# First attention layer: the small term of k's normalization is added to k's squares by GpSimd and VectorE instead of by a second TensorE product

## The chip, the cores and the metric

The kernel runs on one core of a Trainium2 chip. A core has five engines with queues of their own, which wait for each other through semaphores: TensorE (PE in the profile, its weight loads PEld), VectorE (DVE), ScalarE (ACT), GpSimd (POOL) and SyncE (SP), which here issues the DMAs. The metric is the device time of one execution in microseconds; a kernel's time is the median of its runs.

## The reference: what is computed

Four layers over 1040 tokens (16 learned ones and 1024 given) of width 1024: attention over a sliding window, mLSTM, HGRN2, and attention again. Each layer normalizes its input, projects it, mixes it along the sequence, gates the result and projects it back. What matters here is the beginning of an attention layer:

```python
def rmsnorm(x, g):
    xf = x.astype(jnp.float32)
    y = xf * lax.rsqrt(jnp.mean(xf * xf, axis=-1, keepdims=True) + EPS)
    return (y * g.astype(jnp.float32)).astype(x.dtype)
...
    q, k, v, z = _split(u @ w_in, (A_W, A_KVW, A_KVW, A_W))
    q = rope(rmsnorm(q.reshape(bsz, lp, A_HEADS, A_HD), q_gain), pos)
    k = rope(rmsnorm(k.reshape(bsz, lp, A_KV, A_HD), k_gain), pos)
    v = v.reshape(bsz, lp, A_KV, A_HD)
    o = sliding_window_attention(q, k, v, sinks, valid)
```

`u` is the normalized input, so each token's row of it has a factor 1/sqrt(m + EPS), m the mean of the squares of the token's 1024 values. There are 16 heads of q and 4 of k and v, 64 wide. q and k are normalized once more for each head, which takes the token's factor out again except in the small term: with k computed from the input without the token's factor, the mean of k's squares over a head has EPS (m + EPS) added instead of EPS.

## The kernel before

The values lie transposed, 128 channels on the partitions and tokens along the row; `x` has eight such tiles. Tokens are worked in three chunks of 400, 384 and 256. A product of two float32 matrices is made as three products of split values (`uh`, `ul` of the input, `wh`, `wl` of the weights), so one projection of 128 outputs and one chunk is 24 products (L233) that accumulate in one bank `pj`. Weights come by DMA into `wr` (L209), are split by ACT (`wh`, L197) and DVE (`wl`, L198).

The first layer doesn't wait for its own normalization. `Scale.unit` multiplies the input by the gain alone, and the projections start. `Scale.squares` adds up the squares of `x` over the eight tiles in `acc`, one row `r` of the whole length, and `Scale.sums` makes from it, with a product by ones (`pr`), the token's factor, which goes to DRAM (`dram[0]`) for the gates, and EPS m, the small term of the title, which is kept in `acc` and goes to DRAM too (`dram[1]`, tile name `scaled`, L443).

The two tiles of k (two heads each) are made by `qk_proj` with t None. The first tile stands at the layer's head, after the first two tiles of q; the second one (called with fetched=True) stands among the attention units, at some 225 us. For each chunk: `evac` reads the projection out of `pj` with ACT, once with the gain (dst, L577) and once squared (sq, L578); `turned` issues four DMAs that copy quarters of dst, turned by 32 partitions, into a third tile `rot` (L571); `stat` multiplies sq by a mask of ones for each head (L617), which gives every partition the sum of its head's 64 squares, and in this layer adds the small term with a second product (L620), a row of ones with one partition times the row e; `rstd_from` makes 1/sqrt of it on ACT with a logarithm and an exponential (L344, L345); `rope` turns dst with the factors `cs` on DVE (L627 to L631), and `k_split` splits the result (L510 to L513).

For the first tile e is row 0 of `acc`. For the second tile, `acc` being gone, `early` has row 0 of `rot` filled with e from DRAM (L565) while the projection runs, and `turned` comes in `stat`, behind the second product, since it overwrites that row.

The attention then runs in units of one block of 128 queries, two heads: `S_step` (products `pm`, L729 and L730, then a masked maximum on DVE, L737, an exponential on ACT, L740, a reciprocal on DVE, L742, and a multiplication on GpSimd, L743), `T_step` two units later on PE (transposition `pt`, L758) and `V_step` (products `po`, L776). Projections of the next tiles are woven between these steps.

The order on PE is that of a list of steps which the program writes: each step has a cost, and the delays in tables such as `D_K0` and `D_K1` say how long after the end of its projection a step is put in (ns of the list's costs). The order on the other engines is made by a scheduler from the program's order and its own estimates; `hi` gives a step a higher priority there. SP issues its DMAs strictly in its queue's order.

## Time and profile before

| | |
|---|---|
| runs, median (lowest to highest) | 2572.62 us (2570.91 to 2580.6), 3 runs |
| the profiled execution | 2572.24 us, of it the span 2570.4 us |
| PE busy | 2525.0 us, 98% of the span |
| DVE, ACT, POOL busy | 2029.8, 1747.3, 247.6 us |
| granted TensorE clock, mean | 0.999 |
| first layer | from 0 to about 479 us, when the second layer's first products start |
| first k tile, mask products (L617) | at 30.4, 47.1 and 59.4 us |
| first attention unit (L729) and first transposition (L758) | at 63.6 and 67.3 us |
| second k tile, mask products | at 230.7, 236.8 and 243.4 us |

A row of the timeline gives the start in us from the span's start, the duration, engine, line, operation, the names and the shapes; in brackets behind it stands how long the engine was idle before it and what it waited for. Groups of rows give a count, the busy time, the mean duration in ns and the idle time in front. The small product of float32 values appears as two instructions (x2), since it is run in parts. A matmul's end is modelled, and products overlap, so starts are compared and not durations.

### The profile page before, as it was taken

What the parts mean: (1) busy time and instruction counts of PE and PEld (TensorE: products, weight loads), DVE (VectorE), ACT (ScalarE), POOL (GpSimd) and SP (SyncE); (2) the same over time, 40 slices, a digit from 0 to 9 for tenths busy, and PEclk for the clock granted to TensorE, in tenths of its full rate; (3) what the DMA queues carried; (4) which work ended last, traced back from release to release, by engine and by line L of the source; (5) the groups of instructions that cost most, each with busy time, mean ns of one, the idle gap of its engine ahead of it and who ended that gap; (6) DMA issues with size and microseconds to landing.
All of it is one profiled execution on the core that took longest, in us unless ns stands there. A gap on an engine that the chain in (4) does not pass through costs nothing. (4 is left out here: it accounts for less than half of the span.)

```text
span 2570.4 us, 55467 instructions
## 1 busy us (share of the span) xinstructions
PE 2525.0 (98%) x20614; PEld 2476.9 (96%) x20614; DVE 2029.8 (79%) x5602; ACT 1747.3 (68%) x4699; POOL 247.6 (10%) x572
## 2 busy tenths in 40 slices
PE   9999999999999999999999999999999999999999
PEld 8899989999999999999999999999999998999999
DVE  7897898786767676767677788988878888887896
ACT  8766766676565656565675758877676857767772
POOL 0321231000000000000000000110010000321320
PEclk9999999999999999999999999999999999999999
DMA  5223212022222212121221111111111013212112
GB/s 158 63 66 89 60 50 70 30 54 54 48 53 47 50 50 46 53 47 46 50 50 53 56 42 35 35 35 35 43 35 42 27 52 97 61 49 78 55 43 77
DMA packets 103344, 140.27 MB, mean 55 GB/s; under 512 B 15369, under 2 KB 58514, under 8 KB 103074
## 3 DMA queue, kind: packets, MB, share of 16 engines
q1 hardware_dynamic: 103074, 136.73, 19.6%
q8 instruction: 162, 2.65, 0.5%
q14 instruction: 108, 0.88, 0.1%
HBM read 121.83 MB, written 4.27 MB: 49 GB/s over the span
## 5 line engine op out<-in xcount | busy, mean ns | idle before, releaser
L233 PE MATMUL pj<-uh,wh 128*128 128x384 f32 (+2 forms) x2688 | 901.2, 335 | 6.8 <-ACT uh L403 6.3
L233 PE MATMUL pj<-ul,wh 128*128 128x384 f32 (+2 forms) x2688 | 863.5, 321 | 0.3
L233 PE MATMUL pj<-uh,wl 128*128 128x384 f32 (+2 forms) x2688 | 863.0, 321 | 0.0
L233 PEld LDWEIGHTS pj<-uh,wh 128*128 128x128 f32 x2688 | 507.0, 189 | 14.4 <-ACT uh L403 6.3
L233 PEld LDWEIGHTS pj<-ul,wh 128*128 128x128 f32 x2688 | 507.5, 189 | 4.3 <-DVE ul L198 0.9
L233 PEld LDWEIGHTS pj<-uh,wl 128*128 128x128 f32 x2688 | 506.5, 188 | 0.0
L198 DVE TENSOR_TENSOR wl<-wr,wh 128x512 fp32r<-128x512 f32 (+1 forms) x338 | 234.2, 704 | 71.0 <-ACT wh L197 68.5
L197 ACT CAST wh<-wr 128x512 fp32r<-128x512 f32 (+1 forms) x338 | 203.4, 613 | 92.3 <-PE pj L328 34.6
L328 PE MATMUL pj<-yh,wh 128*128 128x384 f32 (+2 forms) x768 | 252.9, 329 | 10.2 <-DVE x L331 8.3
L331 DVE TENSOR_TENSOR x<-x,pj 128x384 f32<-128x384 f32 (+2 forms) x480 | 234.6, 510 | 34.4 <-PE pj L328 33.1
L328 PE MATMUL pj<-yl,wh 128*128 128x384 f32 (+2 forms) x768 | 245.9, 320 | 0.0
L328 PE MATMUL pj<-yh,wl 128*128 128x384 f32 (+2 forms) x768 | 245.8, 320 | 0.0
L283 PE MATMUL pj<-wh,uh 128*128 128x256 f32 (+1 forms) x768 | 222.0, 289 | 0.6 <-DVE kwl L1051 0.6
L283 PE MATMUL pj<-wl,uh 128*128 128x256 f32 (+1 forms) x768 | 216.2, 282 | 0.0
L283 PE MATMUL pj<-wh,ul 128*128 128x256 f32 (+1 forms) x768 | 215.7, 281 | 0.0
L740 ACT ACTIVATE Sm<-Sm,s 128x257 f32<-128x257 f32 (+2 forms) x272 | 131.1, 483 | 88.5 <-DVE s L737 85.8
L743 POOL TENSOR_TENSOR Sm<-Sm,s 128x512 f32<-128x512 f32 (+2 forms) x136 | 139.3, 1025 | 402.9 <-DVE s L742 381.0
L460 ACT ACTIVATE t<-t 128x384 f32<-128x384 f32 (+2 forms) x240 | 118.2, 493 | 66.9 <-DVE t L459 65.5
L197 ACT CAST yh<-r 128x384 fp32r<-128x384 f32 (+2 forms) x120 | 56.9, 479 | 152.3 <-PE pj L328 136.4
L328 PEld LDWEIGHTS pj<-yh,wh 128*128 128x128 f32 x768 | 144.5, 188 | 14.3 <-DVE x L331 10.5
L283 PEld LDWEIGHTS pj<-wh,uh 128*128 128x128 f32 x768 | 144.6, 188 | 1.5 <-DVE kwl L1051 0.9
L328 PEld LDWEIGHTS pj<-yl,wh 128*128 128x128 f32 x768 | 144.6, 188 | 0.6 <-DVE yl L198 0.2
(332 smaller groups left out, 5688.0 us busy)
## 6 DMA issues: line engine op xcount, KB each, us to landing
wr<-in_b_win SPq DMA_DIRECT2D x124, 256.0 KB, 2.9
wr<-in_a_win SPq DMA_DIRECT2D x80, 256.0 KB, 2.8
wr<-in_c_win SPq DMA_DIRECT2D x64, 256.0 KB, 2.8
wr<-in_a_wout SPq DMA_DIRECT2D x32, 256.0 KB, 2.9
rw<-rowsd SPq DMA_DIRECT2D x64, 128.0 KB, 4.7
wr<-in_b_wout SPq DMA_DIRECT2D x32, 256.0 KB, 2.8
t<-t SPq DMA_DIRECT2D x100, 48.0 KB, 1.9
cs<-in_rope SPq DMA_DIRECT2D x11, 400.0 KB, 3.5
```

The lines of the kernel that those rows point to most:

```text
L197: s.copy(h, src)
L198: v.tensor_tensor(l, src, h.bitcast(F32), op=ALU.subtract)
L233: pe.matmul(acc[:, :cn], a[:, k, :], b[:, k, c0 : c0 + cn], start=(k == 0 and i == 0), stop=(k == KT - 1 and i == 2))
L283: pe.matmul(acc[:cn, :nc], a[:, k, c0 : c0 + cn], m[:, kk, :], start=(k == 0 and j == 0), stop=(k == KT - 1 and j == 2))
L328: pe.matmul(acc[:, :cn], a[:, k, mc], b, start=(k == 0 and i == 0), stop=(k == 1 and i == 2))
L331: v.tensor_tensor(x[:, m, c0 : c0 + cn], x[:, m, c0 : c0 + cn], acc[:, :cn], op=ALU.add)
L460: s.activation(a[:, :cn], a[:, :cn], AF.Exp)
L740: s.activation(Sm[:nq, u, : nk + 1], Sm[:nq, u, : nk + 1], AF.Exp, scale=-1.0, bias=st[:nq, u : u + 1], accum_out=den[:nq, u : u + 1])
L743: g.tensor_tensor(Sm[:nq, :, :nk], Sm[:nq, :, :nk], den[:nq].rearrange("p (u c) -> p u c", c=1).to_broadcast([nq, 2, nk]), op=ALU.mult)
```

## The change

The second product goes. `sums` now writes EPS m, without the factor 64, into all 128 rows of `acc` instead of one, and the term is added to the squares before the mask product, which sums 64 of them. A new step `bounded` does that: for the first tile GpSimd adds `acc` to sq; for the second tile the row is read from DRAM into all 128 partitions of `rot`, DVE adds it to sq, and `turned` follows the add, no longer the products. `D_EPS` puts this step 2600 ns and 300 ns behind the projection, ahead of `stat`; for the second tile it has the higher priority. The cost of `stat` in the list is halved, which shifts what is woven around it.

```diff
+D_EPS = 2600.0, 300.0
...
                 pe.matmul(pr[:, :cn], ones, acc, start=True, stop=True)
-                s.activation(acc[0:1], pr[0:1, :cn], AF.Identity, scale=64 * EPS / D)
+                s.activation(acc, pr[:, :cn], AF.Identity, scale=EPS / D)
...
             def early(n, c0, cn):
                 late[n] = work(n, c0, cn)
-                sp.dma_start(late[n][2][0:1], scale.dram[1, c0 : c0 + cn])
+                sp.dma_start(late[n][2], scale.dram[1, c0 : c0 + cn].partition_broadcast(P))
...
                     st = psa()
-                    pe.matmul(st[:, :cn], R["masks"][:, 0:P], sq, start=True, stop=not scaled)
-                    if scaled:
-                        e = late[n][2] if fetched else scale.row[:, c0 : c0 + cn]
-                        pe.matmul(st[:, :cn], ones[0:1], e[0:1], start=False, stop=True)
+                    pe.matmul(st[:, :cn], R["masks"][:, 0:P], sq, start=True, stop=True)
+                    rstd_from(st, sq, cn, 64, scale.eps2 if scaled else eps)
+
+                def bounded():
+
+                    sq = late[n][1]
                     if fetched:
+                        v.tensor_tensor(sq, sq, late[n][2], op=ALU.add)
                         turned(n)
-                    rstd_from(st, sq, cn, 64, scale.eps2 if scaled else eps)
+                    else:
+                        g.tensor_tensor(sq, sq, scale.row[:, c0 : c0 + cn], op=ALU.add)
...
-                return [(d[0], [(8 if scaled else 4) * cn * MM, stat, None]), (d[1], [0.0, rope, None]), (d[2], turn)]
+                res = [(d[0], [4 * cn * MM, stat, None]), (d[1], [0.0, rope, None]), (d[2], turn)]
+                return [(D_EPS[fetched], [0.0, hi(bounded) if fetched else bounded, None])] + res if scaled else res
```

On DVE, at the first attention unit (`pm_848` and `Sm_849` are its products and its probabilities, ISA its maximum, `qs` q's split parts, `v` parts of v, `wl` weights), there stood before:

```order
L530 TENSOR_TENSOR qs_786<-Ph_669,qs_786 64x256
L737 ISA Sm_849,s_851<-pm_848,masks_186,cons_188,rq_404 16x16
L737 ISA s_851 16x1
L690 SCALAR_TENSOR_TENSOR v_833<-pt_824,scale,v_833 128x128
L737 ISA Sm_865,s_867<-pm_864,masks_186,cons_188,rq_404 16x16
L737 ISA s_867 16x1
L737 ISA Sm_849,s_851<-pm_848,masks_186,cons_188,rq_415 16x16
L737 ISA s_851 16x1
L690 SCALAR_TENSOR_TENSOR v_836<-pt_824,scale,v_836 128x128
L737 ISA Sm_865,s_867<-pm_864,masks_186,cons_188,rq_415 16x16
L737 ISA s_867 16x1
L742 RECIPROCAL s_852<-s_852 16x2
```

And in the changed kernel, from the same place on:

```order
L743 ISA Sm_849,s_851<-pm_848,masks_186,cons_188,rq_405 16x16
L743 ISA s_851 16x1
L743 ISA Sm_849,s_851<-pm_848,masks_186,cons_188,rq_416 16x16
L743 ISA s_851 16x1
L531 TENSOR_TENSOR qs_794<-Ph_669,qs_794 64x256
L696 SCALAR_TENSOR_TENSOR v_833<-pt_824,scale,v_833 128x128
L199 TENSOR_TENSOR wl_785<-wr_790,wh_784 128x512
L696 SCALAR_TENSOR_TENSOR v_836<-pt_824,scale,v_836 128x128
L748 RECIPROCAL s_852<-s_852 16x2
L531 TENSOR_TENSOR qs_797<-Ph_669,qs_797 64x256
```

The first unit's maxima moved ahead of the q splits, the second unit's (`Sm_865` before) went behind the first one's reciprocal, and a weight split stands ahead of that reciprocal, where it was the row after it.

On SP, in the second k tile (`scaled` is the row of the small term, t with 32 rows the turned quarters, `wr` weights, `cs` the rope factors), the queue was before:

```order
L587 DMA cs_3196<-in_rope 128x2x400
L565 DMA t_3161<-scaled 1x384
L571 DMA t_3111<-t_3109 32x400 x2
L571 DMA t_3161<-t_3159 32x384 x3
L571 DMA t_3111<-t_3109 32x400
L209 DMA wr_3422<-in_a_win 128x512
L209 DMA wr_3426<-in_a_win 128x512
L587 DMA cs_3258<-in_rope 128x2x384
L565 DMA t_3209<-scaled 1x256
```

And now:

```order
L588 DMA cs_3206<-in_rope 128x2x400
L572 DMA t_3111<-t_3109 32x400 x4
L566 DMA t_3166<-scaled 128x384
L210 DMA wr_3417<-in_a_win 128x512
L210 DMA wr_3421<-in_a_win 128x512
L588 DMA cs_3268<-in_rope 128x2x384
L572 DMA t_3166<-t_3164 32x384 x4
L566 DMA t_3214<-scaled 128x256
```

The row for a chunk now stands behind all four turned quarters of the chunk before, and the read of the rope factors stands ahead of the third row as it did.

## The prediction

> **What bounds the kernel now.** I read the page first, then the waits of TensorE (PE) in the stretch where both k tiles are made, then the stretches around them, then the rows of the removed product.

> ```profile
> span 2570.4 us, 55467 instructions
> PE 2525.0 (98%) x20614; PEld 2476.9 (96%) x20614; DVE 2029.8 (79%) x5602; ACT 1747.3 (68%) x4699; POOL 247.6 (10%) x572
> ```

> PE is busy for 98% of the span, so 45.4 us are all that could be won by removing waits; work taken from PE itself counts where PE does not stand still right after it. Between 20 and 480 us PE waits mostly for transpositions, and once in the second k tile:

> ```profile
> PE pt L758 <- POOL Sm L743: 7.7, 8, 2.2
> ...
> PE pa L617 <- ACT t L578: 1.5, 1, 1.5
> ```

> By stretches (columns: us, busy us of PE, PEld, DVE, ACT, POOL, then the granted clock):

> ```profile
> 20.00:62.00 42.00, 41.91 (x263) 38.23 (x262) 33.45 (x76) 37.74 (x103) 1.17 (x7) 1.00 0.38 106
> ...
> 68.70:72.10 3.40, 3.07 (x16) 2.78 (x15) 2.10 (x6) 2.32 (x6) 1.08 (x3) 0.50 0.81 239
> ```

> While the first k tile is made (20 to 62 us), PE is the bound: 41.91 of 42.00 us. ACT with 37.74 and DVE with 33.45 are close behind, and will not follow all of what PE gains. The granted clock is 0.50 from 68.7 to 72.1 us, after the first long wait of PE, which costs some 1.7 us of the 3.4.

> **The six products removed.** The first chunk of the first k tile, and the same step in the last attention layer, which has no second product and is followed by the same 384 columns:

> ```profile
> 30.36 0.83 PE L617 MATMUL pa<-r,masks 128*128 128x400 f32 x2
> 31.12 0.93 PE L620 MATMUL pa<-r,ones 1*128 1x400 f32 x2
> 31.98 0.44 PE L233 MATMUL pj<-uh,wh 128*128 128x384 f32 x1
> 32.26 0.34 PE L233 MATMUL pj<-ul,wh 128*128 128x384 f32 x1
> ...
> 2135.12 0.83 PE L617 MATMUL pa<-r,masks 128*128 128x400 f32 x2
> ...
> 2135.97 0.34 PE L233 MATMUL pj<-ul,wh 128*128 128x384 f32 x1
> ```

> From the start of the mask product to the second projection product it takes 32.26 - 30.36 = 1.90 us with the second product and 2135.97 - 2135.12 = 0.85 without: 1.05 us. The same for 256 columns, the third chunk of the second k tile against the last layer:

> ```profile
> 243.39 0.70 PE L617 MATMUL pa<-t,masks 128*128 128x256 f32 x2 [1.53 <-ACT t L578]
> 244.02 0.69 PE L620 MATMUL pa<-t,ones 1*128 1x256 f32 x2
> ...
> 244.92 0.34 PE L233 MATMUL pj<-ul,wh 128*128 128x384 f32 x1
> ...
> 2155.55 0.59 PE L617 MATMUL pa<-r,masks 128*128 128x256 f32 x2
> ...
> 2156.15 0.33 PE L233 MATMUL pj<-ul,wh 128*128 128x384 f32 x1
> ```

> 1.53 - 0.60 = 0.93 us. With 1.0 between them for 384 columns, a tile gives 1.05 + 1.0 + 0.93 = 3.0 us, both 6.0. The lower bound takes only the distance from one product's start to the next, 31.12 - 30.36 = 0.76 and 244.02 - 243.39 = 0.63, with 0.7 between: 2.1 a tile, 4.2 in all. I take 3.0, as those rows have the same neighbours. Writing all 128 rows at L442 instead of one keeps the number of columns; I cost it at nothing.

> **The add on GpSimd (first tile).** GpSimd's adds in the trace, and one beside DVE work:

> ```profile
> L743 POOL TENSOR_TENSOR Sm<-Sm,s 128x512 f32<-128x512 f32 x112 | 124.2, 1109 | 259.3 <-DVE s L742 239.5 <-PE pt L758 5.9 <-DVE rq L605 5.1
> ...
> L743 POOL TENSOR_TENSOR Sm<-Sm,s 128x288 f32<-128x288 f32 x16 | 11.1, 694 | 131.9 <-DVE s L742 129.8 <-PE pt L758 2.0
> ...
> 223.28 1.40 POOL L743 TENSOR_TENSOR Sm<-Sm,s 128x512 f32<-128x512 f32 x1 [5.01 <-DVE s L742]
> ...
> 223.89 1.77 DVE L530 TENSOR_TENSOR qs<-t,qs 64x384 fp32r<-64x384 f32 x2
> ...
> L530 DVE TENSOR_TENSOR qs<-t,qs x90: 418/553/1297, 35.5 to 2441.2; 64x384 fp32r<-64x384 f32 x46, 64x256 fp32r<-64x256 f32 x30, 64x400 fp32r<-64x400 f32 x14
> ```

> Between 694 ns (288 columns) and 1109 ns (512), 400 columns take about 0.90 us, 384 about 0.87, 256 about 0.63. Side by side the two engines hold each other up: 1.40 us instead of 1.11 for GpSimd, 0.89 each instead of 0.55 for DVE, so one such add can cost DVE 2 x 0.34 = 0.7 us. [...] Does PE wait for the add? The tightest chunk is the third:

> ```profile
> 55.63 0.36 ACT L578 ACTIVATE r<-pj 128x256 f32<-128x256 f32 x1
> ...
> 59.38 0.59 PE L617 MATMUL pa<-r,masks 128*128 128x256 f32 x2
> ```

> The square ends at 55.99, the add 0.63 later at 56.6, and PE, some 2.05 us earlier after two removed products, comes at 57.3. 0.7 us are left, or 0.4 with the 0.3 us of contention. Cost 0, as long as that cover holds.

> **What the first tile's 3.0 us are worth.** The next thing PE waits for is the first transposition of probabilities, and its chain runs over DVE, ACT and GpSimd:

> ```profile
> 67.32 0.39 PE L758 MATMUL pt<-ident,Sm 128*16 128x128 f32 x2 [2.17 <-POOL Sm L743]
> ...
> 75.48 0.66 PE L758 MATMUL pt<-ident,Sm 128*128 128x128 f32 x4 [0.94 <-POOL Sm L743]
> ...
> 46.45 0.17 DVE L605 SCALAR_TENSOR_TENSOR rq<-pa,scale 128x6 f32<-128x6 f32 x1 [2.39 <-PE pa L600]
> ...
> 63.59 0.87 DVE L530 TENSOR_TENSOR qs<-Ph,qs 64x256 fp32r<-64x256 f32 x2
> ...
> 66.51 0.66 DVE L198 TENSOR_TENSOR wl<-wr,wh 128x512 fp32r<-128x512 f32 x1
> ```

> DVE last waited long for PE at 46.45 us, and there PE is one product (1.05 us) earlier; from then on DVE is nearly full, so it comes forward by 1.05 us, not by 3.0. In the new order the two maxima of the first unit stand ahead of the q splits (0.87 us), but a weight split (0.66 us) now stands ahead of the reciprocal: 1.05 + 0.87 - 0.66 = 1.26 us earlier, so the transposition runs at about 66.1. PE would be there at 67.32 - 2.17 - 3.0 = 62.2 and waits 3.9 us instead of 2.17. Behind it up to the third transposition (75.48) PE has as many rows as before, and the third unit's maxima now go ahead of the splitting of k's last chunk, so of its wait of 0.94 us all may go: 1.26 + 0.94 = 2.2 us. Bounds: 0 (GpSimd's add beside DVE eats the 1.26) and the whole 3.0. I take 2.2. That the wait leaves the clock low is nothing new: it was at 0.50 for 3.4 us already.

> **What the second tile is worth.** SP's queue and the chunks' squares:

> ```profile
> 225.12 0.38 SPq L565 DMA_DIRECT2D t<-scaled  x1
> ...
> 236.99 0.25 SPq L565 DMA_DIRECT2D t<-scaled  x1
> ...
> 238.84 2.43 SPq L571 DMA_DIRECT2D t<-t  x4
> ...
> 243.96 0.38 SPq L587 DMA_DIRECT2D cs<-in_rope  x1
> ...
> 235.29 0.57 DVE L627 TENSOR_TENSOR t<-t,cs 128x400 f32<-128x400 f32 x1 [3.63 <-DMA t<-t]
> ...
> 227.20 0.50 ACT L578 ACTIVATE t<-pj 128x400 f32<-128x400 f32 x1
> ...
> 242.95 0.38 ACT L578 ACTIVATE t<-pj 128x256 f32<-128x256 f32 x1
> ...
> t<-scaled SPq DMA_DIRECT2D x8, 200.0 KB, 3.3
> t<-scaled SPq DMA_DIRECT2D x8, 192.0 KB, 3.1
> t<-scaled SPq DMA_DIRECT2D x8, 128.0 KB, 3.0
> ```

> The row is now spread over 128 partitions, 200 KB for the first chunk; such transfers exist in the gate projections and land after 3.0 to 3.3 us. On the old clock: issued at 225.12, landed 228.4, later than the square (227.7); the add takes a DVE operation of this size (0.57), 229.0. Only then do the four turning transfers go (2.43 us of SP), and behind them in the queue the next chunk's row: 231.4, landed 234.5, added 235.1, turned 237.5; the third row goes at 237.5, lands 240.5, is added at about 241.0. PE, two products earlier, is at the third mask product at 243.39 - 1.53 - 2.05 = 239.8 and waits 1.3 us to 241.1. Before it went at 243.39 because the square (242.95) needed a buffer that the first chunk's k held; that chunk is done sooner, since all its turning transfers no longer wait for PE to read the row out of the same tile. So 243.39 - 241.1 = 2.3 us, and 0.93 for the third product: 3.2. Bounds: 3.0 + 1.5 = 4.5 if no wait is left, 0.9 if the third chunk is not released sooner than now. The three adds on DVE (1.5 us) are covered by its wait of 3.63 us in this stretch; with that cover gone they would sit ahead of the rope work of k, which nobody needs for several us.

> **Sum.** 2.2 + 3.2 = 5.4 us off the profiled execution, whose own time is 2572.24 us (span 2570.4 and 1.8 around it), 0.4 under the median of the runs, 2572.62. That gives 2566.8 on its clock and 2567.2 as a median; I say 2567.

> **Rivals.** 1. All of it counts: 6.0 us of products, 1.5 of the wait at 243.39, and the first transposition follows PE because DVE's chain was itself paced by PE. 2572.6 - 7.5 = 2565, and 2564 with the 0.94 of the third transposition. For it speaks PE's 41.91 of 42.00 us; against it ACT's 37.74 in that stretch. 2. The gain turns into waits: the first transposition stays at 67.3 because GpSimd's adds hold DVE up (0.7 us each), and the third chunk's row lands no earlier than its square came; what is left is about 1 us, 2571.5. [...] 3. Slower: the spread row is held in SP's queue. Ahead of the third row stands the read of the rope factors for the chunk before, and such a read was held until 243.96 us here. If it were so held now, the four turning transfers (2.4) and the row (3.0) would put the add at about 249.8 and the mask product at 249.9: 6.5 us later than now, less 0.93 and the first tile's 2.2, 3.4 us slower, 2576. It decides from an issue of the third row after about 243.1 us; now it is 236.99. 4. That the change doesn't do what it says can be left out: the order has no second product, three adds on GpSimd and three on DVE.

> **How the numbers follow.** A measurement of this kernel tells some 0.5% (13 us) from no change; every case lies inside. Forecast 0.55 (its own range 2564 to 2570), all of it 0.13, turned into waits 0.18, slower 0.14. The range 2562.5 to 2574 leaves out the slower case and the far end of the first rival, under 0.2. Beyond 0.5% on either side I see only what I have not thought of, 0.03 and 0.03.

> **What would show it.** Mask product to second projection product in 0.85 us for 400 columns; the first transposition near 66 us with a wait near 3.9; the third mask product of the second tile near 243.4 - 2.2 - 2.3 = 238.9 us, waiting for a DVE add; from 480 us on no difference in length. Wrong would make it: a mask product of the first tile waiting for GpSimd, SP's third spread row issued after the 243 us mark, or new waits of PE among the units of the first pair.

## The result, and the profile after

The changed kernel takes 2581.77 us (median of 14 runs) where the kernel before takes 2575.40 (14 runs of the same measurement): a ratio of 1.0023, 95% interval 1.0016 to 1.0030. It is slower by some 6 us, where 2567 was forecast. Of all runs on record two were far slower than the others, one of the kernel before (2933.55 us) and one of the second experiment's (7708.59 us); no ratio and no mean below holds them.

The page of the changed kernel, first its span and busy times, then TensorE's waits from 20 to 480 us (us in all, times, longest):

```profile
span 2578.6 us, 55434 instructions
PE 2525.7 (98%) x20602; PEld 2481.9 (96%) x20602; DVE 2035.2 (79%) x5605; ACT 1747.0 (68%) x4699; POOL 250.5 (10%) x575
```

```profile
PE pt L764 <- POOL Sm L749: 6.8, 7, 2.2
PE pa L618 <- DVE t L625: 4.0, 2, 2.7
PE pm L735 <- DVE Pl L767: 4.0, 2, 2.5
...
PE pa L436 <- ACT r L345: 1.1, 1, 1.1
```

Six products are gone, and yet PE is busy for 0.7 us longer than before (2525.7 against 2525.0) and idle for more besides. Where that comes from is seen in the granted clock, the column behind POOL's. These are stretches of 3.41 us of the changed kernel, in pairs: one in which PE waited long, and the one right behind it (columns as in the prediction: us, busy us of PE, PEld, DVE, ACT, POOL, the granted clock, then the DMA's share and GB/s).

```profile
63.40:66.81 3.41, 1.18 (x13) 0.98 (x12) 3.08 (x14) 3.41 (x15) 0.46 (x2) 1.00 0.25 76
66.81:70.22 3.41, 3.41 (x19) 3.27 (x18) 2.40 (x12) 2.32 (x11) 0.42 (x2) 0.50 0.56 158
240.89:244.31 3.42, 1.21 (x7) 1.19 (x8) 1.81 (x4) 2.15 (x6) 0.00 (x0) 1.00 0.83 246
244.31:247.72 3.41, 3.41 (x14) 3.22 (x14) 1.15 (x3) 3.05 (x8) 0.00 (x0) 0.50 0.14 38
329.64:333.06 3.42, 0.89 (x5) 0.57 (x5) 3.30 (x8) 1.52 (x5) 1.46 (x2) 1.00 0.41 138
333.06:336.47 3.41, 3.41 (x15) 3.39 (x14) 2.76 (x10) 1.10 (x4) 0.42 (x1) 0.50 0.03 7
401.32:404.74 3.42, 1.34 (x12) 1.13 (x11) 3.36 (x10) 3.37 (x11) 1.14 (x1) 1.00 0.03 8
404.74:408.15 3.41, 3.41 (x17) 3.41 (x18) 2.44 (x9) 2.33 (x8) 0.36 (x2) 0.50 0.02 5
2445.91:2449.32 3.41, 1.25 (x9) 0.98 (x8) 3.32 (x8) 1.01 (x4) 1.09 (x2) 1.00 0.01 2
2449.32:2452.73 3.41, 3.41 (x15) 3.41 (x14) 2.53 (x8) 0.00 (x0) 0.00 (x0) 0.50 0.00 0
```

Five times PE works at half clock (0.50) for 3.41 us and loses some 1.7 us each time, an estimate that takes half of the 3.41 us; the profile of before shows this once. The starts of the five, 66.81, 244.31, 333.06, 404.74 and 2449.32 us, lie 52, 26, 21 and 599 times 3.413 us apart: a grid that holds over these 2382.51 us, 698 times 3.413. One 3.413 us stretch of it is called a field here. The wait of about 2.1 us near 400 us stands in both kernels. In the changed one it falls into one field of the grid (2.08 us of idle time) and the next field is at half clock; in the kernel before a border of the grid cuts it into 1.11 and 0.98 us, and the clock stays at 1.00:

```profile
396.40:399.81 3.41, 2.30 (x20) 2.10 (x18) 3.28 (x12) 3.35 (x10) 0.21 (x1) 1.00 0.21 37
399.81:403.23 3.42, 2.44 (x20) 2.44 (x21) 3.25 (x11) 3.02 (x9) 1.11 (x2) 1.00 0.02 5
```

In the five fields ahead of the half-clock stretches PE was idle for 2.08 to 2.53 us.

The grid doesn't stand at the same place in every execution: counted from the span's start, a border lies at 68.72 us in the profile of before and at 66.81 in that of the changed kernel, 1.91 us apart, which is less than a field. And the executions of one kernel don't lose the same: the mean granted clock of the 14 runs of the changed kernel lies between 0.993 and 0.998. What all runs have is the mean granted clock c of the span. The time lost to the half clock is put at (1 - c) times the span, and the rest at what the kernel would take at full clock. Means over the runs of each kernel (over all kernels of this document the standard error is 0.4 to 1.1 us for the lost time and 0.3 to 0.6 for the last column; c is known to three digits in each run):

| kernel | mean us | lost to half clock | at full clock |
|---|---|---|---|
| before (33 runs, first experiments) | 2576.5 | 5.3 | 2571.2 |
| changed (14 runs) | 2582.0 | 10.9 | 2571.1 |

By this reckoning the change is worth nothing at full clock, and it doubles what the half clock takes, by 5.6 us. That is the result in two numbers; the experiments have to say why.

The reckoning is good to 1 or 2 us. The kernel before has no c on record for its 14 runs beside the changed kernel; their mean is 2575.7, 0.8 under that of the 33. And within one kernel, over the 221 runs of this document with a c, a run that lost 1 us more by c was only 0.74 us longer (standard error 0.04; the rounding of c explains a part of what is missing to 1). At that price 4.1 of the 5.5 us between the two rows are the half clock's, and the change costs 1.4 us at full clock.

### The profile page after: what moved, and what is told of

The parts are those of the page before. It is cut to its first block, busy times and chain, and to the rows that moved or that the text cites. A ratio compares the mean times of both kernels' runs of the same rounds, so it can differ in the third digit from the quotient of the medians.

```text
span 2578.6 us, 55434 instructions
## 1 busy us (share of the span) xinstructions
PE 2525.7 (98%) x20602; PEld 2481.9 (96%) x20602; DVE 2035.2 (79%) x5605; ACT 1747.0 (68%) x4699; POOL 250.5 (10%) x575
## 4 chain that ended last, share of the span: by engine, by line
PE 76%; DVE 10%; ACT 8%; DMA 3%; issue 2%; POOL 0%; SPq 0%; DVEq 0%; ACTq 0%; POOLq 0%
PE pj L234 37%; PE pj L329 16%; PE pj L284 9%; PE po L1015 2%; PE po L782 2%; PE pt L764 1%; DVE wl L199 1%; ACT Sm L746 1%; DVE Sm L743 1%; PE pm L1358 1%; ACT wh L198 1%; PE pm L735 1%; PE pm L736 1%; DMA rw<-rowsd 1%; PE pj L280 1%
## 5 line engine op out<-in xcount | busy, mean ns | idle before, releaser
L234 PEld LDWEIGHTS pj<-uh,wh 128*128 128x128 f32 x2688 | 508.0, 189 | 12.8 <-ACT uh L404 6.6
L198 ACT CAST wh<-wr 128x512 fp32r<-128x512 f32 (+1 forms) x338 | 203.1, 613 | 91.1 <-PE pj L329 33.8
L198 ACT CAST yh<-r 128x384 fp32r<-128x384 f32 (+2 forms) x120 | 56.9, 479 | 153.3 <-PE pj L329 139.1
L329 PEld LDWEIGHTS pj<-yh,wh 128*128 128x128 f32 x768 | 145.1, 189 | 12.8 <-DVE x L332 7.7
## 6 DMA issues: line engine op xcount, KB each, us to landing
rw<-rowsd SPq DMA_DIRECT2D x64, 128.0 KB, 4.5
```

Source lines behind the costliest of these rows:

```text
L198: s.copy(h, src)
L234: pe.matmul(acc[:, :cn], a[:, k, :], b[:, k, c0 : c0 + cn], start=(k == 0 and i == 0), stop=(k == KT - 1 and i == 2))
L329: pe.matmul(acc[:, :cn], a[:, k, mc], b, start=(k == 0 and i == 0), stop=(k == 1 and i == 2))
```

## The experiments

Three theories were in question. A: the new order costs the time. The mask product's step is entered in the list at cost 4 instead of 8, so the interleaving of the projections with the attention steps shifts in many places. B: the second tile's spread rows and adds cost it. C: a long wait costs a half-clock stretch beside itself, and whether it does depends on the grid. The tables give means as above; ratios are those of the measurement, each against the kernel before.

**1. The adds in the old order.**

```
-  res = [(d[0], [4 * cn * MM, stat, None]), ...
+  res = [(d[0], [(8 if scaled else 4) * cn * MM, stat, None]), ...
```

> The changed kernel with one number put back: the step of the mask product is again entered in the list with the cost of two products (8 instead of 4 per column), so TensorE's instructions stand in the order of the kernel before, but without the second products and with the three GpSimd and three VectorE adds. Theory A (the new order costs the time): waits at 330 us and 620 us go, TensorE's idle time from 260 to 700 us falls from 15.9 us back to about 12, and the time is 1 to 4 us below the kernel before. Theory B (the second tile's rows and adds cost the time, the order is harmless): the two waits for VectorE's adds near 235 and 240 us stay at 1.3 and 2.7 us, and the time stays 4 to 7 us above the kernel before. Theory C (clock gate): whatever the time, every stretch at half clock is 3.41 us long, all of them lie on one grid of 3.413 us, and each follows a grid window in which TensorE stood idle for 2.0 us or more.

Measured: 2576.96 us, ratio 1.0005 (0.9996 to 1.0013). TensorE's waits from 20 to 480 us:

```profile
PE pa L618 <- DVE t L625: 3.1, 2, 2.0
PE pm L735 <- DVE x L332: 1.7, 1, 1.7
```

With the old order no loss clear of the noise is left, so A holds as to sign; but the gain of 1 to 4 us that A expected isn't there in the time. The wait near 330 us is back at 1.66 us, that for VectorE's adds stays (3.1 us), and the idle time from 260 to 700 us is 12.8 us, close to the 12 of before. Its profile has five half-clock stretches on one grid, each behind a field with 1.92 to 2.21 us of idle time, so the 2.0 of C was set too high. At full clock the kernel is at 2569.2, 2.0 under before; the half clock takes 7.7 instead of 5.3.

**2. The new order alone.**

```
-  (d[0], [(8 if scaled else 4) * cn * MM, stat, None])
+  (d[0], [4 * cn * MM, stat, None])          # in the kernel before
```

> The kernel before with that one number changed (cost 4 instead of 8): six second products as before, no adds, one-row reads, but TensorE's order of the changed kernel. Theory A: 4 to 8 us slower than the kernel before, with a wait above 2.2 us near 330 us and one near 620 us. Theory B: within 2 us of the kernel before, third mask product of the second tile waiting some 1.5 us or less. Theory C as above: half-clock stretches only after grid windows with at least 2.0 us of idle time.

Measured: 2582.11 us, ratio 1.0023 (1.0013 to 1.0033), the same as for the whole change and inside A's 4 to 8 us. One number of the list, with no instruction added or removed on TensorE, costs what the change costs. The row near 330 us in the kernel before, and here:

```profile
330.28 0.39 PE L729 MATMUL pm<-r,qs 128*128 128x256 f32 x1 [1.68 <-DVE x L331]
```

```profile
335.37 0.58 PE L729 MATMUL pm<-r,qs 128*128 128x256 f32 x1 [2.52 <-DVE Pl L761]
```

In the new order the step of the scores (S) stands one projection step earlier there. It waits for VectorE, which comes no sooner, so 0.85 us of covered waiting turn into an open wait; and 2.52 us are enough for a half-clock stretch where 1.68 were not: in the profiles of the five kernels with the second tile's new cost (the changed one, experiments 2, 4, 5 and 9) the wait is 2.5 us, and a half-clock stretch begins each time within 1 us of the wait's end; in the other eight it is 1.6 to 1.7 us and none begins there.

A second place lies near 160 us. The changed kernel's VectorE has a row of a gate (L479) between the two maxima (L743) for which a transposition waits, 1.22 us; in the kernel before the two maxima (L737) stand together, and the wait is 0.17 us:

```profile
159.09 0.54 DVE L743 CUSTOM_DVE_ANT_0 Sm<-pm,masks,cons 128x256 f32<-128x256 f32 x1
...
159.55 0.56 DVE L479 TENSOR_TENSOR r<-r,t 128x384 f32<-128x384 f32 x1
160.02 0.54 DVE L743 CUSTOM_DVE_ANT_0 Sm<-pm,masks,cons 128x256 f32<-128x256 f32 x1
```

```profile
160.75 0.54 DVE L737 CUSTOM_DVE_ANT_0 Sm<-pm,masks,cons 128x256 f32<-128x256 f32 x1
...
161.21 0.54 DVE L737 CUSTOM_DVE_ANT_0 Sm<-pm,masks,cons 128x256 f32<-128x256 f32 x1
```

It is so in all kernels in which the first tile has cost 4, and also in the tenth experiment, where TensorE's order is the old one: this place hangs on VectorE's order, which a scheduler makes, and so only in part on the cost. At full clock the order costs 1.3 us (2572.5), by the half clock 4.5 more (9.8 lost).

The wait near 620 us that A named isn't there: its 2.25 us stood in the profile of the changed kernel alone, and no other kernel's profile has more than 1.21 us at that place.

**3. The change on the first tile alone.**

```
-  sp.dma_start(late[n][2], scale.dram[1, c0 : c0 + cn].partition_broadcast(P))
+  sp.dma_start(late[n][2][0:1], scale.dram[1, c0 : c0 + cn])   # row 64 times as large
 ...
+  if scaled and fetched:
+      pe.matmul(st[:, :cn], ones[0:1], late[n][2][0:1], start=False, stop=True)
+      turned(n)
```

> The change on the first k tile alone: GpSimd adds there, the second tile has its one-row read and its second product as before (the row in DRAM is written 64 times as large by one small ACT operation per chunk). Theory A: still slower or even, since half of the order's change is in it, -1 to +3 us. Theory B: the first tile gains what three products are worth, 2 to 3 us faster than the kernel before, no wait for a VectorE add at 235 and 240 us.

The step has cost 4 for the first tile and 8 for the second here. Measured: 2576.83 us, ratio 1.0007 (0.9997 to 1.0017). As far as the time goes, A's range holds it and B's does not. At full clock it is level with the first experiment (2568.8 against 2569.2; 2.4 under before), but it loses 9.2 us to the half clock. One of its waits is for GpSimd's add itself:

```profile
47.98 1.21 POOL L633 TENSOR_TENSOR r<-r,r 128x384 f32<-128x384 f32 x1 [17.89 <-ACT r L581]
```

```profile
49.24 1.65 PE L620 MATMUL pa<-r,masks 128*128 128x384 f32 x2 [2.38 <-POOL r L633]
```

ACT makes the second chunk's square some 6 us later here than in the changed kernel, the add comes after it, and PE stands in front of the mask product; a half-clock stretch starts at 49.13 us.

**4. The change on the second tile alone.**

```
-  pe.matmul(st[:, :cn], R["masks"][:, 0:P], sq, start=True, stop=True)
+  pe.matmul(st[:, :cn], R["masks"][:, 0:P], sq, start=True, stop=not scaled or fetched)
+  if scaled and not fetched:
+      pe.matmul(st[:, :cn], ones[0:1], scale.row[0:1, c0 : c0 + cn], start=False, stop=True)
```

> The change on the second k tile alone: spread rows and VectorE adds there, the first tile has its second product (the row in DRAM is written 1/64 as large by one small ACT operation per chunk). Theory A: 0 to +4 us. Theory B: 6 to 9 us slower than the kernel before, with waits for VectorE's add near 1.3 us at the second and 2.7 us at the third chunk, the third spread row landing 3.9 us after its issue as in the changed kernel.

The step has cost 8 for the first tile and 4 for the second here. Measured: 2579.51 us, ratio 1.0012 (1.0004 to 1.0021). The waits for VectorE's add are 1.68 and 2.71 us (B: 1.3 and 2.7), but the loss is 3 us and not 6 to 9; A's 0 to 4 holds it. At full clock 2573.5, 2.3 over before: what the first tile gains (2.4) the second loses, each with its part of the new order in it.

**5. The new order without the adds.**

```
-  v.tensor_tensor(sq, sq, late[n][2], op=ALU.add)
   turned(n)
-  else: g.tensor_tensor(sq, sq, scale.row[:, c0 : c0 + cn], op=ALU.add)
-  sp.dma_start(late[n][2], scale.dram[1, c0 : c0 + cn].partition_broadcast(P))
```

> The changed kernel, in its own order, with the small term left out of k's squares altogether: no adds on GpSimd or VectorE and no spread rows for the second tile (so k's factor lacks the entry's small term; the rest is computed as before). Theory A (the order costs 5 to 6 us, the six products are worth about what the second tile's waits take back): the two waits at 235 and 240 us (4.0 us together) go, the wait of 2.5 us near 330 us stays; 2 to 5 us under the changed kernel, so between the kernel before and 4 us above it. Rival (the adds cost nothing on the path): within 1 us of the changed kernel, some 6 us above the kernel before.

Measured: 2581.85 us, ratio 1.0016 (1.0008 to 1.0025). In microseconds the median is that of the changed kernel, but the kernel before was slower in this measurement: against it the loss is 4.7 us, over A's 0 to 4 and under the rival's 6. So the time decides neither; the parts say more. At full clock it is 2.3 under before, where the changed kernel is 0.1 under, so the adds and rows do cost some 2 us on the path; but it loses 11.7 us to the half clock. Its profile has the wait near 330 us (2.51), the third transposition's (2.15, as in the second experiment), and, since PE no longer waits in the second tile, 1.80 us at v's transposition behind it, at 247.7 us; the changed kernel has less than 0.8 at the last two. Work taken away ahead of a wait came out as a longer wait.

**6. Idle products in the kernel before.**

```
+  for _ in range(FILL[first].get((w["pair"], b, w["hh"]), 0)):
+      pe.matmul(pt[:, 0, 0, :], ident, ident, start=True, stop=True)
   for ki, (kb, ko, _) in enumerate(kbs):      # the transpositions
```

> The kernel before with 12 idle products of TensorE (identity by identity, 128 columns, into the tile that the transpositions then overwrite), placed ahead of three transpositions for which TensorE waits about 2 us each: 5 at 65 us, 4 at 399 us, 3 at 2181 us. Theory C (a grid window of 3.41 us with about 1.9 us or more of idle time is followed by one at half clock): no half-clock stretch at 68, 400 or 2184 us in any execution; the waits become 0.6 to 0.9 us shorter each with the transposition at the same time; median 1.5 to 4 us under the kernel before. Rival (the half clock costs nothing, or does not follow from the idle time): no change, or up to 1 us slower by the added products.

Measured: 2575.91 us against 2577.16, ratio 0.9993 (0.9984 to 1.0001). Smaller than expected, and the interval just reaches no change. The profile has no half-clock stretch at the three filled places; it has others (75.0, 245.7, 2153.7, 2447.3 us). The transposition runs at 67.34 us, where it ran at 67.32 without the products, with half the wait:

```profile
65.00 1.27 PE L754 MATMUL pt<-ident 128*128 128x128 f32 x10
67.34 0.39 PE L762 MATMUL pt<-ident,Sm 128*16 128x128 f32 x2 [1.06 <-POOL Sm L744]
```

The lost time falls from 5.5 us to 3.7, and at full clock nothing changes (2571.5 both).

**7. The same, with the adds in the old order.** As the sixth, on the first experiment's kernel, and ahead of the second tile's mask products:

```
   st = psa()
+  for _ in range((0, 4, 3)[n] if fetched else 0):
+      pe.matmul(st[:, :P], ident, ident, start=True, stop=True)
   pe.matmul(st[:, :cn], R["masks"][:, 0:P], sq, start=True, stop=True)
```

> The adds in the order of the kernel before (the first experiment's kernel), with idle products ahead of the first transposition (6), the second and third mask product of the second k tile (4 and 3), and the transpositions at 397 us (4) and in the last attention layer (3). Theory C: the half-clock stretches at 65, 236, 400 and 2185 us go and only one near 2444 us can remain; 3 to 6 us under the kernel of the first experiment, so 2571 to 2574 where the kernel before has 2576.7. Rival: no change against the first experiment.

Measured: 2572.11 us against 2577.16, ratio 0.9985 (0.9976 to 0.9994): 4.9 us under the kernel of the first experiment. The lost time falls from 7.7 to 3.3 us. The profile has one half-clock stretch that C didn't want, right behind a wait of 2.43 us at the third mask product that three products didn't fill.

**8. The second tile's rows read by GpSimd's queue.**

```
-  sp.dma_start(late[n][2], scale.dram[1, c0 : c0 + cn].partition_broadcast(P))
+  g.dma_start(late[n][2], scale.dram[1, c0 : c0 + cn].partition_broadcast(P))
```

> The first experiment's kernel with the second tile's three spread rows read by GpSimd's queue instead of SP's, where they stand behind the four turning transfers of the chunk before and ahead of weights and rope factors. Theory (SP's queue sets the chain): the rows land before the squares, the waits of 1.96 and 1.18 us at the second and third mask product fall to under 0.5 us each, and the time is 1 to 4 us less than in the first experiment. Rival (the spread transfer itself, or the release of its buffer, sets the chain): waits as before, no change in time.

Measured: 2580.00 us, ratio 1.0014 (1.0005 to 1.0023), and not the gain of the theory. The rival had the cause, the release of a buffer, though not the waits, which move into one:

```profile
PE pa L618 <- DVE t L625: 6.1, 1, 6.1
```

```profile
233.84 0.54 POOL L566 DMA_DIRECT2D t<-scaled  x1 [5.42 <-DVE t L634]
```

```profile
241.11 0.39 ACT L579 ACTIVATE t<-pj 128x256 f32<-128x256 f32 x1 [1.80 <-DVE t L634]
242.18 0.42 DVE L625 TENSOR_TENSOR t<-t,t 128x256 f32<-128x256 f32 x1
```

The wait at the second mask product is gone, and the third has all of it and more. The third row goes only when VectorE's rope work (L634) frees its buffer, and the third chunk's square waits for the next such release, in turn for the rope factors of the chunk before. So SP's queue set the second chunk's time, and in this kernel the six temporary buffers set the third's.

**9. Idle products in the changed kernel.** As the seventh, in the new order, with 5, 2, 6, 4 and 3 products.

> The changed kernel, in its own order, with idle products ahead of the first transposition (5), the second and third mask product of the second k tile (2 and 6), the transposition at 403 us (4) and the first one of the last attention layer (3). The wait of 2.5 us at 330 us, which comes from the order, can't be filled in this way and stays. If half-clock stretches after long waits are a part of the changed kernel's loss: 3 to 5 us under the changed kernel, so 0 to 3 us above the kernel before, with half-clock stretches left at 333 us (in most executions) and near 2449 us. Rival (the order's loss is all plain waiting): within 1 us of the changed kernel, 5 to 6 us above the kernel before.

Measured: 2577.83 us against 2578.88, ratio 0.9992 (0.9983 to 1.0001), where the changed kernel had 1.0023. By the ratios twenty idle products take back 0.3% or 8 us, more than the 3 to 5 expected (by the means, each against its own kernel before, 7.1). They bring the changed kernel level, within the noise, with the filled kernel before of the sixth experiment (0.9992 and 0.9993; 20 and 12 idle products): with most of the long waits filled, no loss by the change is left. The lost time falls from 10.9 to 6.1 us, below that of the kernel before in this measurement (6.8). The wait that the order made stays, and so does the half-clock stretch behind it, at 333.19 us:

```profile
332.29 0.39 PE L738 MATMUL pm<-r,qs 128*128 128x256 f32 x1 [2.52 <-DVE Pl L773]
```

**10. The first tile alone, in the old order, filled.** The third experiment's kernel with cost 8 for both tiles and 6, 3, 4 and 3 idle products.

> GpSimd's adds on the first k tile alone, in the order of the kernel before (cost 8 kept for both tiles), the second tile with its one-row read and second product, and idle products ahead of the first transposition (6), the third mask product of the second tile (3), the transposition near 399 us (4) and the first one of the last attention layer (3). If the first tile's three products are worth 2.6 us, as the first experiment's trace has it, and the second tile's 1.2: 2570 to 2573 where the kernel before has 2577, within 1.5 us of the seventh experiment. Rival (the gain of the seventh experiment came from the second tile): 2574 or more.

Measured: 2574.74 us against 2578.88, ratio 0.9986 (0.9977 to 0.9995). As a ratio it equals the seventh. In microseconds it falls in the rival's range (2574 or more); but the kernel before was at 2578.9 and not at 2577 in this measurement, and 4.1 us under it is the near edge of the 4 to 7 expected. So the time alone doesn't settle it. At full clock it is 2.0 under before.

**11. More idle products in the seventh.**

```
-  for _ in range((0, 4, 3)[n] if fetched else 0):
+  for _ in range((0, 5, 7)[n] if fetched else 0):
```

> The seventh experiment's kernel with 5 and 7 instead of 4 and 3 idle products at the second and third mask product of the second k tile, where its trace still had a wait of 2.43 us and a half-clock stretch right behind it. Theory C: that stretch goes in all executions, which is worth 0.57 x 1.7 = 1 us over the seventh experiment, and its slowest executions (2577) come down to 2573. Rival: the added products themselves hold TensorE up, and the time is the same or up to 1 us more.

Measured: 2570.64 us against 2578.88, ratio 0.9969 (0.9958 to 0.9979): 8 us faster than the kernel before, and the best of all. By the ratios that is 4 us over the seventh, where 1 was expected; the two intervals just overlap. It loses 1.8 us to the half clock.

```profile
PE pt L770 <- POOL Sm L752: 5.2, 7, 1.4
PE pj L330 <- DVE x L333: 3.3, 4, 1.6
PE pa L621 <- DVE t L628: 2.4, 2, 1.3
```

No wait up to 480 us is longer than 1.7 us now. Its slowest run still took 2577 us, so C's "in all executions" is too strong: in its profile two fields behind 2153 us were at half clock although PE was idle for only 0.7 us in the field ahead (more on that in the last section).

All kernels together:

| kernel | ratio | lost to half clock | at full clock, against before |
|---|---|---|---|
| changed (lost and full clock against the first 33 runs) | 1.0023 | 10.9 | -0.1 |
| 1 adds, old order | 1.0005 | 7.7 | -2.0 |
| 2 new order alone | 1.0023 | 9.8 | +1.3 |
| 3 first tile | 1.0007 | 9.2 | -2.4 |
| 4 second tile | 1.0012 | 6.1 | +2.3 |
| 5 new order, no adds | 1.0016 | 11.7 | -2.3 |
| 6 before, filled | 0.9993 | 3.7 | 0.0 |
| 7 adds, old order, filled | 0.9985 | 3.3 | -1.7 |
| 8 rows by GpSimd | 1.0014 | 11.3 | -2.3 |
| 9 changed, filled | 0.9992 | 6.1 | -0.9 |
| 10 first tile, old order, filled | 0.9986 | 4.4 | -2.0 |
| 11 as 7, more filled | 0.9969 | 1.8 | -2.6 |

The kernel before lost 5.3, 5.5 and 6.8 us in the three measurements (1 to 4, 5 to 8, 9 to 11). Read as steps at full clock, the order costs 1.3 (2), the removed products then give 3.6 (from 2 to 5, each against its own before), and adds and rows take 2.2 back (from 5 to the changed kernel): -0.1 in all. Each step has a standard error of 0.6 to 0.8 us; with 0.74 us for each lost one they would be 2.5, 3.1 and 2.0, and +1.4 in all. Filling the waits changes the lost time (by 1.7 us in 6, 4.5 and 5.9 in 7 and 11, 4.8 in 9) and leaves the full-clock column within 1 us of the unfilled kernel (6: 0.0; 7 and 11 against 1: +0.3 and -0.6; 9 against the changed one: -0.8). So between kernels that differ by idle products, 1 us less lost is about 1 us less time; in these pairs the half clock follows from the waits, and 1.7 to 5.9 us of it were taken away by themselves.

## Why the prediction was wrong

**The products removed: right in size, wrong as time.** The mask product of 400 columns starts at 31.24 us and the second projection product at 32.09, the 0.85 us that were named:

```profile
31.24 0.83 PE L618 MATMUL pa<-r,masks 128*128 128x400 f32 x2
31.60 0.65 PE L234 MATMUL pj<-uh,wh 128*128 128x384 f32 x1
32.09 0.33 PE L234 MATMUL pj<-ul,wh 128*128 128x384 f32 x1
```

Of the 6.0 us only 3.6 (standard error 0.8) come out at full clock without any add, from experiment 2 to 5.

**The add on GpSimd at cost 0.** It holds for the changed kernel: no mask product of the first tile waits for GpSimd. The estimates of 0.90, 0.87 and 0.63 us were low; the adds took 1.03, 1.30 and 0.73. The cover is thin: in the third experiment it was gone, and PE waited 2.38 us, in the tenth 1.33. What wasn't seen is another wait in that stretch, 1.12 us at 50.5 us for ACT (L345, in the rows above), which takes half of what two removed products give (2.05 us). The text had said that ACT would not follow all of it, and put no number to it.

**The first transposition: right; the wait ahead of it, not.** It runs at 66.34 us, where about 66.1 was named. But PE waits 2.23 us there and not 3.9, since it comes later than thought: the first mask product is at 31.24 instead of 30.36 (it lies anywhere from 30.1 to 31.7 in the profiles), and then the 1.12 us for ACT. The first tile's 2.2 us: in the old order they are there. From the first mask product of the first tile to that of the second it takes 200.3 us in the kernel before and 197.7 in the first experiment, each with one half-clock stretch in it: 2.6 us. In the changed kernel it takes 198.5, and between two transpositions around 160 us (142.4 to 172.2 us, before 145.0 to 173.1) 29.8 us instead of 28.0: 1.8 us went there, 1.2 of them as the wait for the two maxima. That cost stood in no step.

**The second tile: wrong sign.** The mechanism, the chain of spread row, add and turning transfers through SP's queue, was right; its durations were not. SP's and VectorE's rows of the changed kernel:

```profile
223.93 0.51 SPq L566 DMA_DIRECT2D t<-scaled  x1
...
231.04 0.95 SPq L566 DMA_DIRECT2D t<-scaled  x1
...
238.64 0.58 SPq L566 DMA_DIRECT2D t<-scaled  x1
```

```profile
242.52 0.43 DVE L625 TENSOR_TENSOR t<-t,t 128x256 f32<-128x256 f32 x1 [1.28 <-DMA t<-scaled]
```

```profile
243.10 0.67 PE L618 MATMUL pa<-t,masks 128*128 128x256 f32 x2 [2.73 <-DVE t L625]
```

The third row went at 238.64 us instead of 237.5 and the three took 3.9, 4.5 and 3.8 us to land, not 3.3, 3.1 and 3.0 as the equal transfers of the gate projections. The mask product came at 243.10, where 241.1 on the old clock, or 238.9 with the first tile's gain, was named. The "gain" of 3.2 us is a loss of 2.3 at full clock with the order in it (fourth experiment), and behind the wait of 2.73 us, against 1.53 before, stands a half-clock stretch, from 244.31 us on.

**From 480 us on no difference.** To about 2 us this holds at full clock: from the first product of the next layer to PE's end it takes 2088.1 us before and 2089.3 to 2091.6 in the profiles of the changed kernel and the experiments 1 to 4, with one or two half-clock stretches (1.7 us each) in these and none in that of before. The stretches themselves are the exception that the prediction didn't have.

**The sum.** This is the step that failed. It was made on a profiled execution with one half-clock stretch, and took this for a fixed part of the kernel ("that the wait leaves the clock low is nothing new"). The kernel before loses 5.3 us to half-clock stretches on the mean, that execution 1.7 by its one stretch, and the changed one 10.9. The term that was put at nothing, the change of this loss, is +5.6 us; two more, the order and the second tile's adds and rows, made the rest of the sum come to -0.1 instead of -5.4. The base was low too: the three runs shown had a median of 2572.62, fourteen have 2575.40. Together the 5.3 between -5.4 and -0.1, the 5.6 and the 2.8 of the base are 13.7 us, the most part of the 14.8 between 2567.0 and 2581.8. (With 0.74 us for each lost one the half clock's term is 4.1 and the rest of the sum +1.4.) Nor does the kernel need 13 us to be told from no change, as the prediction had it: the interval of the ratio is 1.8 us to either side.

**The rivals.** The first, that all of it counts, fell with the waits of 2.23 us at 66.34 and 2.73 us at 243.10. The second (the gain turns into waits) was right in kind, though the first transposition ran at 66.34 us and not at 67.3; its 2571.5 us has nothing of the 5.6 us that the half clock took besides. The third needed the row to go after about 243.1 us; it went at 238.64 and didn't come to pass. That the list's cost, changed in the same line, moves the order and costs time by itself was seen in the order and priced at the first attention unit alone; the waits near 330 and 160 us were in no rival.

## What to carry to other kernels

A wait of TensorE of about 2 us cost more than itself in these kernels, since the work behind it could run at half clock for 3.41 us (so it did behind all 38 fields with 1.86 us or more of idle time): count the waits that a change lifts to that length, and compare kernels by the mean granted clock of many runs and by the time at full clock, not by one profile. Where a wait can't be removed, a few idle products into a tile that is overwritten anyway brought back a part of that loss: 1.7 of 5.5 us in the sixth experiment, 4.8 of 10.9 in the ninth, 5.9 of 7.7 in the eleventh. And a cost in a scheduling list is a change of its own: try it alone before it is taken along with another.

## What the runs showed of the hardware

```profile
2151.62 0.39 PE L235 MATMUL pj<-uh,wh 128*128 128x256 f32 x1
2152.08 0.39 PE L235 MATMUL pj<-ul,wh 128*128 128x256 f32 x1
```

Counted in columns of products that start in a field, all 49 half-clock fields that stand behind one at full clock follow one with 3072 columns or fewer, every field with 2304 or fewer (31) is followed by one, and between the two 18 of 37. For scale, an estimate from the 384-column products ahead of the row at 31.24 us, which start 0.175 us apart (30.71, 30.88, 31.06): a field full of them would hold some 7,500. No run set the columns or the idle time by itself, so it isn't shown which of the two the half clock follows.
